# Decoder trunk: the merge's broadcast loads on GpSimd's queue, the output projection's residual and sum of squares on VectorE, and a reordered pool

## The chip, the cores and the metric

The kernel runs on one core of a Trainium2 chip. The metric is device microseconds (us) of one execution. A core has TensorE (PE in the profile, its weight loads PEld), VectorE (DVE), ScalarE (ACT), GpSimd (POOL) and SyncE (SP). Each engine works through its own instructions in their order. SP does nothing but issue DMAs here; POOL issues DMAs too and computes a little. A DMA issued by either engine is one in that engine's queue: an issue that has to wait for a semaphore holds up all that stands behind it on its engine.

## The reference

One pre-norm block on x (2048 tokens, 1024 channels, fp32), a ReLU-squared MLP and a final norm:

```python
u = _rmsnorm(h, norm_mix_g[l])
z = jnp.einsum('bsd,dn->bsn', u, w_in[l])
q, k, v, pz, ga, gp = jnp.split(z, offs, axis=-1)
a = _attention_branch(q, k, v)          # 3 head groups (dilation 1, 4, 16), 4 heads of 64 each
p = _pool_branch(pz, w_pool_grp[l], pool_scale[l])
merged = sigmoid(ga) * (a @ w_att_out[l]) + sigmoid(gp) * (p @ w_pool_out[l])
h = h + merged @ w_out[l]
m = _rmsnorm(h, norm_mlp_g[l])
h = h + square(relu(m @ w_mlp_in[l])) @ w_mlp_out[l]
return _rmsnorm(h, norm_final_g)
```

In `_attention_branch` the outputs of the three groups are added with weights: the softmax, over the groups, of the log-sum-exp of each head's scores at each token.

## The kernel before

All products are in fp32 accuracy: each operand is split into a high and a low part (ScalarE casts the high part, VectorE subtracts for the low one, L527 and L528), and a product is three matmuls (L534 to L536). Tokens are cut into 4 chunks of C = 512, or into 2 halves of 1024. The parts in order of time:

- Queries, keys and values of group 2, the pool branch and the attention of group 2 (until about 420 us).
- A loop over the 4 chunks (L398 to L502, about 420 to 890 us): projections and attention blocks of groups 1 and 0, then the chunk's *merge*. For it VectorE works out the weights on 4 partitions (one for each head), POOL's queue writes them to DRAM (`wts_d`, L486), and six DMAs on SP's queue read them back, each row to 64 partitions (`wb`, L495, one for each of 3 groups and 2 pairs of heads). VectorE multiplies each group's output by its `wb` (L498 for group 0, L500 for the others) and adds up (L501) into `af`, which POOL's queue stores to `a_d` (L502). `wb` has three buffers, so that the fourth load waits until the first buffer has been used.
- The *B part* (L547 to L751, about 890 to 2255 us), with a pool `wp` of its own and the order gates(0), merge(0), gates(1), residual(0), merge(1), mlp_in(0), residual(1), mlp_in(1). Gates, residual and mlp_in run `stage` (L611): a matrix product in Strassen's manner, in rounds of two output pairs j, each with seven products (ORDER1). The first three products of a pair leave PSUM as tiles zA, zS, zS (L637, ScalarE copies); of the next three each is added to one of them on VectorE (L640), the seventh becomes zc, and `fin` does what is left with each of the four results. All these tiles and `fin`'s own come from one ring of buffers, tag zz, ZB = 12 of them. The names of tiles and of PSUM banks carry the stage: g gates, o output projection (residual), c first layer of the MLP; hx, h22 and tt tiles are activations, raw (r_) and s tiles are weights, w and m tiles are their split parts.
- `residual` (the stages o): `fin` adds x to z by a DMA on POOL's queue that accumulates in place (L699), stores h (L700), squares z on ScalarE (L702), adds the square into `hss_d` in DRAM by another accumulating DMA (L703), scales z in place (L704) and stores hg (L705).
- The MLP's second layer and the final norm (pool c2, until the end).

A scheduler with a simulated timeline sets the order of instructions on each engine, by priority and by the times that it works out for them; a tile that takes a buffer over waits for the last use of the tiles that were there. Pools are laid out in SBUF in the order in which tags first appear, so that a tag's place decides which earlier tiles its first buffers lie over.

Of the kernel before, what the change touches and what calls it, by code (L numbers as in the profile page):

```python
# [12 lines left out]
ALU = mybir.AluOpType  # L13
# [6 lines left out]
KD = D // P  # L20
# [27 lines left out]
def trunk_kernel(ctx: ExitStack, tc, xt, w_qk, w_v, w_pz, w_grp, w_gates, w_att, w_pool, w_o, w_1, w_2, cols, out):  # L48
    nc = tc.nc
# [16 lines left out]
    mg_d = dram.tile([KD, P, SEQ], F32, name="mg_d")  # L66
    hg_d = dram.tile([KD, P, SEQ], F32, name="hg_d")
    hss_d = dram.tile([NCH, P, C], F32, name="hss_d")
# [11 lines left out]
    g_mix, g_mlp, g_fin = colt[:, 0:KD], colt[:, KD:2 * KD], colt[:, 2 * KD:3 * KD]  # L80
# [135 lines left out]
    for half in range(2):  # L216
        grp = fold.tile([96, 2, 2, 192], F32, name=f"grp{half}", tag="grp", bufs=2)
        nc.sync.dma_start(grp, w_grp[half])
        for quarter in range(4):
            wz = fold.tile([96, 2, 2, 256], F32, name=f"wz{half}_{quarter}", tag="wz", bufs=4)  # L220
            nc.sync.dma_start(wz, w_pz[half, quarter])
            for k in (2 * quarter, 2 * quarter + 1):
                ps = ps_a1(f"fold{half}_{k}")
# [5 lines left out]
                src = ps[:, :384].rearrange("p (n j) -> p n j", n=3)  # L229
# [11 lines left out]
    with ExitStack() as st:  # L241
        a1 = pool_of(st, "a1")
        wqk, wv = [], []
        for c in range(NCH):
            cs = slice(c * C, (c + 1) * C)
            ssq = a1.tile([P, C], F32, name=f"ssq{c}", tag="ssq", bufs=2)
# [100 lines left out]
    with ExitStack() as st:  # L347
# [4 lines left out]
        for c in range(NCH):  # L352
            u = gained_x(c, f"a2_{c}")
            for n in range(6):
                w = split_load(w_pzg_d[n], D, f"wz{c}_{n}", lo_on=nc.gpsimd)
                ps = ps_mm(f"a2_{c}_{n}")
# [3 lines left out]
                z = zext[n]  # L360
# [37 lines left out]
    for c in range(NCH):  # L398
        u = xh, xl = norm_x(c, f"a3_{c}")
        ot, negm, ll = {}, {}, {}  # L400
        for g in (1, 0):
            qk = []
            for i in range(4):
                w = split_load(w_qk[4 * g + i], D, f"a3_{c}_{g}_{i}")
                ps = ps_mm(f"a3_{c}_{g}_{i}")
                mm3_chunk(ps, w, u)
                t = a3p.tile([P, C], F32, name=f"qk_{c}_{g}_{i}", tag=f"q{g}" if i < 2 else f"k{g}",
                             bufs=2 if i < 2 else 4)
# [8 lines left out]
            for t in range(4):  # L417
                ps = ps_mm(f"a3v_{c}_{g}_{t}")
# [71 lines left out]
        for g in range(3):  # L490
            for hp in range(2):
                wb = mg.tile([P, C], F32, name=f"wb_{c}_{g}_{hp}", tag="wb", bufs=3)
                src = bass.AP(tensor=wts_d.tensor, offset=wts_d[c, g, 2 * hp].offset,
                              ap=[[C, 2], [0, HD], [1, C]])
                nc.sync.dma_start(wb, src)  # L495
                o = (o2c if g == 2 else ot[g])[:, hp, :]
                if g == 0:
                    nc.vector.tensor_mul(af[:, hp, :], wb, o)  # L498
                else:
                    nc.vector.tensor_mul(wb, wb, o)  # L500
                    nc.vector.tensor_add(af[:, hp, :], af[:, hp, :], wb)  # L501
# [46 lines left out]
    wp = pool_of(wps, "wp")  # L548
    COMBS = ("B11", "T1", "T2", "B22", "T3", "B21", "T4")
    ORDER1 = ("A11 B11 b", "S1 T1 c", "S2 T2 b", "S4 B22 c", "S3 T3 b", "A12 B21 a", "A22 T4 b")  # L550
    RAWB, SB, WB, ZB = 4, 5, 5, 12

    def wtile(name, tag="zz", bufs=ZB):
        return wp.tile([P, C], F32, name=name, tag=tag, bufs=bufs)

    def load_act(src, k, t, hf, key, tag="hx", bufs=3):

# [50 lines left out]
            raw.append(r)  # L608
        return [r[:, i * C:(i + 1) * C] for r in raw for i in range(2)]

    def stage(key, weights, n_pairs, make, fin, extra=None):  # L611


        m = {}
        for j0 in range(0, n_pairs, 2):
            js = (j0, j0 + 1)
            w, bank, mid = {}, {}, {}
            for j in js:
                a11, a12, a21, a22 = raws((weights[2 * j], weights[2 * j + 1]), f"{key}_{j}")
                s1, s2, s3, s4 = sums(a11, a12, a21, a22, f"{key}_{j}")  # L620
                w[j] = {"A11": a11, "A12": a12, "A22": a22, "S1": s1, "S2": s2, "S3": s3, "S4": s4}
            for n, step in enumerate(ORDER1):
                a, b, bk = step.split()
                if j0 == 0:
                    m[b] = make(b)
                for j in js:
                    kj = f"{key}_{j}"
                    wh, wl = split(wp, w[j][a], f"{kj}_{a}", "w", WB)
                    first = (j, bk) not in bank
                    if first:  # L630
                        bank[j, bk] = ps_c(f"{kj}_{bk}")
                    ps = bank[j, bk]
                    mm_acc(ps, [(wh[:, k * P:(k + 1) * P], wl[:, k * P:(k + 1) * P], *m[b][k])
                                for k in range(KH)], first, True)
                    if n in (0, 1, 2):
                        t = mid[j, n] = wtile(f"z{a}_{kj}")
                        nc.scalar.copy(t, ps)  # L637
                    elif n < 6:
                        t = mid[j, {3: 2, 4: 1, 5: 0}[n]]
                        nc.vector.tensor_add(t, ps, t)  # L640
                        fin(j, *{3: (0, 1), 4: (1, 1), 5: (0, 0)}[n], t, None)
                    else:
                        fin(j, 1, 0, wtile(f"zc_{kj}"), ps)
            if extra:
                extra(j0 // 2)

    def at(hf, t):
        return slice(hf * HT + t * C, hf * HT + (t + 1) * C)
# [43 lines left out]
                nc.gpsimd.dma_start(mg_d[e, :, at(hf, t)], z)  # L692

    def residual(hf):
        def fin(j, row, t, z, ps):
            e, c = 2 * j + row, 2 * hf + t
            if ps is not None:
                nc.scalar.copy(z, ps)
            nc.gpsimd.dma_start(z, xt[c, :, e, :], accum_op=ALU.add)  # L699
            nc.gpsimd.dma_start(h_d[e, :, at(hf, t)], z)  # L700
            sq = wtile(f"sq_{c}_{e}")
            nc.scalar.square(sq, z)  # L702
            nc.gpsimd.dma_start(hss_d[c], sq, **({"accum_op": ALU.add} if (j, row) != FIRST else {}))  # L703
            nc.scalar.mul(z, z, g_mlp[:, e:e + 1])  # L704
            nc.gpsimd.dma_start(hg_d[e, :, at(hf, t)], z)  # L705

        FIRST = (0, 0)
        stage(f"o{hf}", w_o, KD // 2, inputs(mg_d, hf, f"o{hf}"), fin)


    def mlp_in(hf):
# [217 lines left out]
```

## Time and profile before

| | |
|---|---|
| median of 3 runs | 2917.45 us (2913.21 to 2920.82) |
| profiled execution | 2918.79 us |
| its span | 2916.7 us |
| PE / DVE / ACT / POOL busy, share of the span | 91% / 62% / 46% / 14% |

A row of instructions in the profile's views reads: start or group, engine, line, operation, output<-input by the program's names with the buffer numbers left out, tile sizes, and how often (x). In a timeline the first two numbers are start and duration in us, and square brackets give how long the engine was idle ahead of it and what ended that. A row of waits reads: engine, what it was about to do, what it waited for; us in total, times, longest. A row of windows has the stretch, its length, the busy time of PE, PEld, DVE, ACT and POOL with the number of instructions, the TensorE clock that was granted (1 is 2.4 GHz, 0.5 is 1.2 GHz), the share of the 16 DMA engines' time, and GB/s.

### The profile page before, as it was taken

The page shows a single profiled execution, that of the slowest core. Times are in us where ns is not written, and L with a number is a line of the kernel's source. Part 1 is how long each engine was busy: PE and PEld are TensorE (multiplying, and loading weights), DVE is VectorE, ACT ScalarE, POOL GpSimd, SP SyncE. Part 2 cuts the span into 40 slices and gives each one's busy share as a digit, 9 for nine tenths or more (in the row PEclk, how much of TensorE's full clock was granted, in tenths as well). Part 3 has the DMA queues.
Part 4 walks back from the last instruction along what each step waited for, and adds up shares of the span by engine and source line. Part 5 has one row for each costly group of instructions (what it writes and reads, how often), then busy time and mean ns, then how long its engine had stood idle before and what let it go on. Part 6 is the DMA issues. An engine that isn't in the chain of part 4 may idle for free.

```text
span 2916.7 us, 37152 instructions
## 1 busy us (share of the span) xinstructions
PE 2652.3 (91%) x12966; PEld 2177.2 (75%) x12966; DVE 1815.4 (62%) x2848; ACT 1355.0 (46%) x2504; POOL 405.8 (14%) x617
## 2 busy tenths in 40 slices
PE   8999999788727999997999999769999999999996
PEld 7887788677625887886678887658887788878885
DVE  5469847555447457574576667466665584787557
ACT  5444444334325433454335556455555544464444
POOL 3024300000000110113302221332222000000000
PEclk9999999899868999998899999889999999999998
DMA  7234544422106465357955556785555946683433
GB/s 254 82 111 163 175 171 145 137 80 98 55 24 200 130 228 180 131 186 181 305 183 199 188 188 208 194 222 188 188 188 201 329 124 193 206 268 105 127 111 127
DMA packets 207948, 493.92 MB, mean 169 GB/s; under 512 B 26672, under 2 KB 33840, under 8 KB 207632
## 3 DMA queue, kind: packets, MB, share of 16 engines
q1 hardware_dynamic: 160128, 347.75, 37.7%
q0 software_dynamic: 47632, 143.79, 14.6%
q8 instruction: 102, 1.67, 0.2%
q14 instruction: 86, 0.70, 0.1%
HBM read 347.68 MB, written 143.75 MB: 168 GB/s over the span
## 4 chain that ended last, share of the span: by engine, by line
PE 47%; issue 35%; DMA 9%; DVE 4%; POOL 3%; ACT 1%; SPq 0%; POOLq 0%; DVEq 0%; ACTq 0%
PE z L535 6%; PE z L536 6%; PE z L534 6%; PE z_c_b L534 3%; PE z_c_b L536 3%; PE z_c_b L535 3%; PE z_c_c L534 2%; PE z_c_c L536 2%; PE z_c_c L535 2%; PE mm_v L275 2%; DMA x<-hid_d 1%; POOL sg_d L654 1%; PE mm L125 1%; PE mm L126 1%; PE mm L127 1%
## 5 line engine op out<-in xcount | busy, mean ns | idle before, releaser
L528 DVE TENSOR_TENSOR wl_S<-r_S,wh_S 128x512 fp32r<-128x512 f32 x128 | 88.3, 690 | 123.5 <-ACT wh_S L527 123.5
L527 ACT CAST wh_S<-r_S 128x512 fp32r<-128x512 f32 x128 | 79.9, 624 | 182.1 <-PE z L535 162.6
L535 PE MATMUL z<-xl_T,wh_S 128*128 128x512 f32 x384 | 149.6, 390 | 2.8 <-DVE xl_T L528 2.8
L316 ACT ACTIVATE sb_g<-sb_g,negm 128x256 f32<-128x256 f32 (+1 forms) x192 | 86.2, 451 | 136.4 <-DVE negm L314 136.4
L536 PE MATMUL z<-xh_T,wl_S 128*128 128x512 f32 x384 | 149.4, 389 | 0.0
L528 DVE TENSOR_TENSOR wl_c_S<-s_c,wh_c_S 128x512 fp32r<-128x512 f32 x128 | 86.8, 688 | 94.7 <-ACT wh_c_S L527 94.5
L534 PE MATMUL z<-xh_T,wh_S 128*128 128x512 f32 x384 | 135.7, 389 | 0.0
L527 ACT CAST wh_c_S<-s_c 128x512 fp32r<-128x512 f32 x128 | 77.2, 616 | 75.9 <-PE z_c_c L535 41.0
L321 PE MATMUL t_g<-ident,sb_g 128*128 128x128 f32 x300 | 67.0, 315 | 43.9 <-ACT sb_g L316 43.4
L527 ACT CAST wh_A<-r_A 128x512 fp32r<-128x512 f32 x96 | 59.5, 620 | 98.8 <-PE z L535 62.0
L528 DVE TENSOR_TENSOR wl_A<-r_A,wh_A 128x512 fp32r<-128x512 f32 x96 | 65.8, 687 | 59.2 <-ACT wh_A L527 58.5
L126 PE MATMUL mm_a<-xl_a,hi_a 128*128 128x512 f32 x256 | 102.4, 401 | 0.0
L535 PE MATMUL z<-xl_B,wh_A 128*128 128x512 f32 x256 | 100.5, 393 | 1.5 <-DVE xl_B L528 1.5
L127 PE MATMUL mm_a<-xh_a,lo_a 128*128 128x512 f32 x256 | 101.9, 398 | 0.0
L125 PE MATMUL mm_a<-xh_a,hi_a 128*128 128x512 f32 x256 | 99.8, 398 | 1.4 <-ACT qk L410 1.4
L534 PE MATMUL z<-xh_B,wh_A 128*128 128x512 f32 x256 | 94.2, 400 | 6.5 <-ACT xh_B L527 5.8
L536 PE MATMUL z<-xh_B,wl_A 128*128 128x512 f32 x256 | 98.2, 392 | 0.0
L798 POOL TENSOR_TENSOR y<-y,frs 128x256 f32<-128x256 f32 x4 | 3.2, 825 | 650.9 <-DVE frs L146 650.9
L527 ACT CAST wh_c_A<-r_c 128x512 fp32r<-128x512 f32 x96 | 59.5, 620 | 69.2 <-PE z_c_b L535 27.1
L535 PEld LDWEIGHTS z<-xl_T,wh_S 128*128 128x128 f32 x384 | 72.1, 188 | 18.6 <-DVE xl_T L528 3.7
L528 DVE TENSOR_TENSOR wl_c_A<-r_c,wh_c_A 128x512 fp32r<-128x512 f32 x96 | 65.8, 685 | 29.7 <-ACT wh_c_A L527 29.7
L534 PEld LDWEIGHTS z<-xh_T,wh_S 128*128 128x128 f32 x384 | 72.1, 188 | 15.1
(503 smaller groups left out, 8681.0 us busy)
## 6 DMA issues: line engine op xcount, KB each, us to landing
x<-hid_d SPq DMA_DIRECT2D x160, 256.0 KB
r_c<-in_w SPq DMA_DIRECT2D x64, 512.0 KB
r_S<-w2s_d SPq DMA_DIRECT2D x128, 256.0 KB
x_a<-in_xt SPq DMA_DIRECT2D x96, 256.0 KB
r_A<-in_w SPq DMA_DIRECT2D x96, 256.0 KB
raw_a<-in_w_qk SPq DMA_DIRECT2D x32, 512.0 KB
r_g<-in_w_gates SPq DMA_DIRECT2D x32, 512.0 KB
r_w<-in_w SPq DMA_DIRECT2D x32, 512.0 KB
```

The lines of the kernel that those rows point to most:

```text
L125: nc.tensor.matmul(ps, lh, rh, start=(i == 0), stop=False)
L126: nc.tensor.matmul(ps, lh, rl, start=False, stop=False)
L127: nc.tensor.matmul(ps, ll, rh, start=False, stop=(i == n - 1))
L275: nc.tensor.matmul(pv[t][:, :256], a, b, start=(k == 0 and n == 0), stop=(k == KD - 1 and n == 2))
L316: nc.scalar.activation(s[:, h, :W], s[:, h, :W], AF.Exp, bias=negm[:, col + h:col + h + 1], accum_out=l[:, col + h:col + h + 1])
L321: nc.tensor.transpose(ps_t[:, b, h * P:(h + 1) * P], s[:, h, b * P:(b + 1) * P], ident)
L527: nc.scalar.copy(hi, src)
L528: nc.vector.tensor_sub(lo, src, hi.bitcast(F32))
L534: nc.tensor.matmul(ps, lh, rh, start=start and i == 0, stop=False, skip_group_check=True)
L535: nc.tensor.matmul(ps, lh, rl, start=False, stop=False, skip_group_check=True)
L536: nc.tensor.matmul(ps, ll, rh, start=False, stop=stop and i == n - 1, skip_group_check=True)
L654: nc.gpsimd.dma_start(sg_d[2 * j + row, :, at(hf, t)], z)
```

## The change

1. The 24 `wb` loads (L495) are issued on GpSimd's queue in place of SP's.
2. In `wp` the ring zz has 11 buffers in place of 12, a new tag ssq has two, and both are allocated ahead of all others, so that they take the pool's lowest addresses; raw, s, hx and the rest move up.
3. In `residual`, SP's queue loads the chunk of x into the z tile ahead of the product, and VectorE adds PSUM to it (`onto`; 32 loads and 32 adds), where ScalarE copied PSUM out (32 copies) and POOL's queue accumulated x (32 DMAs). VectorE sums the squares in the ssq tiles (28 adds), with four stores of them to `hss_d`, where 32 DMAs did it. The scaled copy goes to a tile of its own (hg) from zz.

```diff
-                nc.sync.dma_start(wb, src)
+                nc.gpsimd.dma_start(wb, src)
...
-    RAWB, SB, WB, ZB = 4, 5, 5, 12
+    RAWB, SB, WB, ZB = 4, 5, 5, 11
...
+    for tag, bufs in (("zz", ZB), ("ssq", 2)):
+        wtile(f"first_{tag}", tag, bufs)
...
-    def stage(key, weights, n_pairs, make, fin, extra=None):
+    def stage(key, weights, n_pairs, make, fin, extra=None, onto=None):
...
                     if n in (0, 1, 2):
                         t = mid[j, n] = wtile(f"z{a}_{kj}")
-                        nc.scalar.copy(t, ps)
+                        if onto:
+                            nc.sync.dma_start(t, onto(j, *((0, 0), (1, 1), (0, 1))[n]))
+                            nc.vector.tensor_add(t, ps, t)
+                        else:
+                            nc.scalar.copy(t, ps)
...
     def residual(hf):
+        ssq = [wtile(f"ssq_{hf}_{t}", "ssq", 2) for t in range(2)]
+
+        def onto(j, row, t):
+            return xt[2 * hf + t, :, 2 * j + row, :]
+
         def fin(j, row, t, z, ps):
-            e, c = 2 * j + row, 2 * hf + t
+            e = 2 * j + row
             if ps is not None:
-                nc.scalar.copy(z, ps)
-            nc.gpsimd.dma_start(z, xt[c, :, e, :], accum_op=ALU.add)
+                nc.sync.dma_start(z, onto(j, row, t))
+                nc.vector.tensor_add(z, ps, z)
             nc.gpsimd.dma_start(h_d[e, :, at(hf, t)], z)
-            sq = wtile(f"sq_{c}_{e}")
-            nc.scalar.square(sq, z)
-            nc.gpsimd.dma_start(hss_d[c], sq, **({"accum_op": ALU.add} if (j, row) != FIRST else {}))
-            nc.scalar.mul(z, z, g_mlp[:, e:e + 1])
-            nc.gpsimd.dma_start(hg_d[e, :, at(hf, t)], z)
-
-        FIRST = (0, 0)
-        stage(f"o{hf}", w_o, KD // 2, inputs(mg_d, hf, f"o{hf}"), fin)
+            if e == 0:
+                nc.scalar.square(ssq[t], z)
+            else:
+                sq = wtile(f"sq_{hf}_{t}_{e}")
+                nc.scalar.square(sq, z)
+                nc.vector.tensor_add(ssq[t], ssq[t], sq)
+            g = wtile(f"hg_{hf}_{t}_{e}")
+            nc.scalar.mul(g, z, g_mlp[:, e:e + 1])
+            nc.gpsimd.dma_start(hg_d[e, :, at(hf, t)], g)
+
+        stage(f"o{hf}", w_o, KD // 2, inputs(mg_d, hf, f"o{hf}"), fin, onto=onto)
+        for t in range(2):
+            nc.gpsimd.dma_start(hss_d[2 * hf + t], ssq[t])
```

The change moves instructions at three places. First SP's queue at the end of the last chunk's merge, where the first loads of the gates' weights (r_g) and activations (hx_g_B) follow; before:

```order
L488 DMA o2c_7228<-o_d 128x2x512
L495 DMA wb_0_0_7231<-wts_d 128x1x512
L495 DMA wb_0_1_7234<-wts_d 128x1x512
L495 DMA wb_1_0_7237<-wts_d 128x1x512
L495 DMA wb_1_1_7241<-wts_d 128x1x512
L495 DMA wb_2_0_7245<-wts_d 128x1x512
L495 DMA wb_2_1_7249<-wts_d 128x1x512
L607 DMA r_g_0_0_7267<-in_w_gates 128x1024
L607 DMA r_g_0_1_7269<-in_w_gates 128x1024
```

The same place on SP after the change:

```order
L431 DMA v_3_3_6578<-v_d_64 128x256
L488 DMA o2c_7228<-o_d 128x2x512
L611 DMA r_g_0_0_7269<-in_w_gates 128x1024
L611 DMA r_g_0_1_7271<-in_w_gates 128x1024
L611 DMA r_g_1_0_7281<-in_w_gates 128x1024
L611 DMA r_g_1_1_7283<-in_w_gates 128x1024
L563 DMA hx_g_B_0_0_7293<-u_d 128x512
```

Before, the gates' first loads stand behind the six wb loads, which wait for `wts_d`; now they stand behind o2c alone. The wb loads are on POOL's queue now, between the store that they wait for and the store of the merge's result:

```order
L486 DMA wts_d<-nm_7158 4x3x512
L495 DMA wb_0_0_7231<-wts_d 128x1x512
L495 DMA wb_0_1_7234<-wts_d 128x1x512
L495 DMA wb_1_0_7237<-wts_d 128x1x512
L495 DMA wb_1_1_7241<-wts_d 128x1x512
L495 DMA wb_2_0_7245<-wts_d 128x1x512
L495 DMA wb_2_1_7249<-wts_d 128x1x512
L502 DMA a_d<-af_7230 128x1024
```

Only stores of later work stand behind them there. The third place is the first residual stage, from its first round (pairs 0 and 1) to its second (2 and 3); ScalarE before, where the two names of a tile in L704 are one tile:

```order
L702 ACTIVATE sq_1_11185<-zc_o_0_11181 128x512
L698 COPY zc_o_1_11206<-z_o_1_b 128x512
L527 CAST wh_o_2_S_11399<-s_o_2_11221 128x512
L704 ACTIVATE zc_o_0_11181<-zc_o_0_11181,colt 128x512
L702 ACTIVATE sq_3_11210<-zc_o_1_11206 128x512
L637 COPY zA_o_2_11256<-z_o_2_b 128x512
L637 COPY zA_o_3_11275<-z_o_3_b 128x512
```

VectorE at that place after the change:

```order
L720 TENSOR_TENSOR ssq_0_10705<-ssq_0_10705,sq_0_1_11191 128x512
L713 TENSOR_TENSOR zc_o_1_11213<-z_o_1_b,zc_o_1_11213 128x512
L528 TENSOR_TENSOR wl_o_2_S_11328<-s_o_2_11228,wh_o_2_S_11327 128x512
L604 TENSOR_TENSOR s_o_3_11241<-r_o_3_0_11235,r_o_3_1_11237 128x512
L720 TENSOR_TENSOR ssq_0_10705<-ssq_0_10705,sq_0_3_11217 128x512
L528 TENSOR_TENSOR wl_o_3_S_11347<-s_o_3_11240,wh_o_3_S_11346 128x512
L644 TENSOR_TENSOR zA_o_2_11264<-z_o_2_b,zA_o_2_11264 128x512
L644 TENSOR_TENSOR zA_o_3_11284<-z_o_3_b,zA_o_3_11284 128x512
```

What empties the PSUM banks of pairs 2 and 3 (zA_o_2, zA_o_3) stood on ScalarE behind the squares of zc, and stands on VectorE behind the sums now; it also has the load of x as an input.

## Rows read from the trace of the kernel before

**Rows 1.** Page, busy time of TensorE: us, share of the span, instructions.

```profile
PE 2652.3 (91%) x12966; PEld 2177.2 (75%) x12966; DVE 1815.4 (62%) x2848; ACT 1355.0 (46%) x2504; POOL 405.8 (14%) x617
```

**Rows 2.** Waits of TensorE in the whole span.

```profile
PE z_g_b L534 <- ACT mB11h_g L527: 60.3, 1, 60.3
PE t_g L321 <- ACT sb_g L316: 43.4, 10, 8.3
PE z_o_b L534 <- ACT zA_o L637: 26.1, 2, 13.7
PE z_c_b L534 <- ACT zA_c L637: 21.5, 1, 21.5
PE o_g L329 <- ACT ot L331: 16.5, 3, 5.9
```

**Rows 3.** Windows around the merges of chunks 0, 1 and 2.

```profile
500.00:560.00 60.00, 41.75 (x292) 36.41 (x291) 27.85 (x42) 20.78 (x45) 2.37 (x5) 0.83 0.25 85
640.00:680.00 40.00, 21.95 (x149) 20.44 (x150) 14.59 (x24) 11.08 (x27) 1.13 (x2) 0.74 0.24 85
765.00:800.00 35.00, 18.23 (x125) 16.59 (x127) 10.21 (x17) 8.24 (x22) 0.58 (x1) 0.66 0.17 64
```

**Rows 4.** VectorE's waits for tile wb in all four merges: us, times.

```profile
  DMA wb<-wts_d: 109.8, 24
```

**Rows 5.** Timeline of the last chunk's merge and the start of the gates.

```profile
847.04 20.12 SPq L495 DMA_DIRECT2D wb<-wts_d  x6
854.61 0.69 DVE L498 TENSOR_TENSOR af<-wb,ot 128x512 f32<-128x512 f32 x1 [10.51 <-DMA wb<-wts_d]
859.88 0.69 DVE L498 TENSOR_TENSOR af<-wb,ot 128x512 f32<-128x512 f32 x1 [4.58 <-DMA wb<-wts_d]
865.24 0.69 DVE L500 TENSOR_TENSOR wb<-wb,ot 128x512 f32<-128x512 f32 x1 [4.67 <-DMA wb<-wts_d]
...
870.58 0.69 DVE L500 TENSOR_TENSOR wb<-wb,ot 128x512 f32<-128x512 f32 x1 [3.92 <-DMA wb<-wts_d]
...
876.71 0.69 DVE L500 TENSOR_TENSOR wb<-wb,o2c 128x512 f32<-128x512 f32 x1 [5.45 <-DMA wb<-wts_d]
...
884.09 0.69 DVE L500 TENSOR_TENSOR wb<-wb,o2c 128x512 f32<-128x512 f32 x1 [5.48 <-DMA wb<-wts_d]
...
885.13 0.62 ACT L527 CAST wh_g_A<-r_g 128x512 fp32r<-128x512 f32 x1 [49.39 <-DMA r_g<-in_w_gates]
...
890.32 1.22 PE L534 MATMUL z_g_b<-mB11h_g,wh_g_A 128*128 128x512 f32 x2 [60.25 <-ACT mB11h_g L527]
```

**Rows 6.** Window in which little but wb loads moves.

```profile
850.00:870.00 20.00, 0.00 (x0) 0.00 (x0) 2.77 (x4) 0.00 (x0) 0.00 (x0) 0.50 0.13 49
```

**Rows 7.** The accumulating loads of x, L699, POOL's queue: issue to landing.

```profile
DMA to landing us min/median/max: 4.1/7.1/11.1
```

**Rows 8.** The stores u_d, L176, POOL's queue: issue to landing.

```profile
DMA to landing us min/median/max: 2.6/5.1/10.2
```

**Rows 9.** Windows of residual(0), two, and residual(1), two.

```profile
1330.00:1380.00 50.00, 37.60 (x156) 30.57 (x155) 17.76 (x27) 20.96 (x36) 22.61 (x32) 0.86 0.88 210
1380.00:1440.00 60.00, 52.97 (x201) 39.61 (x200) 31.38 (x51) 30.13 (x53) 24.62 (x35) 0.86 0.98 278
1860.00:1900.00 40.00, 26.31 (x110) 21.30 (x109) 11.40 (x17) 18.37 (x33) 15.76 (x23) 0.83 0.89 208
1900.00:1960.00 60.00, 34.91 (x138) 27.69 (x137) 36.52 (x58) 31.12 (x55) 22.50 (x31) 0.78 0.94 245
```

**Rows 10.** ScalarE's timeline in residual(0), ahead of the second round's first copy.

```profile
1371.26 0.63 ACT L702 ACTIVATE sq<-zc_o 128x512 f32<-128x512 f32 x1 [1.59 <-DMA zc_o<-in_xt]
1371.80 1.05 ACT L637 COPY zA_o<-z_o_b 128x512 f32<-128x512 f32 x2
```

**Rows 11.** Start of c2: SP's first weight load, and mlp_in(1)'s last group of stores.

```profile
2241.25 0.33 SPq L763 DMA_DIRECT2D r_A<-in_w  x1
L715 POOL DMA_DIRECT2D hid_d<-zc_c x32: 539/542/542, 1547.9 to 2254.4; - x32
```

## The prediction

> **What bounds the kernel now.** I began with the page's busy times: TensorE works 2652.3 us of the span of 2916.7 [rows 1]. The change takes no matmul away, so it can only win back what TensorE stands idle, 264 us, and what it runs slowly after standing idle. Next I read TensorE's waits. Five groups matter here [rows 2]: one wait of 60.3 us for the gates' first activation; 43.4 us and 16.5 us in the attention loop for ScalarE's exponentials (sb_g) and outputs (ot); 26.1 us in the residual stages and 21.5 us just behind the second, for the copy zA that empties a PSUM bank. Then I asked, by timeline and windows, what stands behind each.
>
> In the attention loop the releaser named is ScalarE, but the cause is VectorE: it works in order, its part of the attention blocks stands among the merge's multiplications, and these wait for wb. The 24 waits for wb sum to 109.8 us [rows 4]. Of these the last merge has six, 10.51 + 4.58 + 4.67 + 3.92 + 5.45 + 5.48 = 34.6 us [rows 5], so each of the others has 75.2 / 3 = 25.1 us. Around those three merges TensorE stands idle 60 - 41.75 = 18.3, 40 - 21.95 = 18.1 and 35 - 18.23 = 16.8 us [rows 3], 53 us together. The granted clock there is 0.83, 0.74 and 0.66, that is 20.4, 20.8 and 23.8 us at the lower level, 65 us in all. If all idle time lay in these, 12 us of work ran at half speed and lost 6 us; if none, 65 us did and lost 32. The middle is 19: the merges cost TensorE 53 + 19 = 72 us.
>
> The 60.3 us are the last chunk's: no next chunk covers its merge. The first wb load is issued at 847.04 and used at 854.61, 7.6 us later, and then one comes every 4.6 to 6.7 us, as if one after another; the last addition ends at 884.81 + 0.69 = 885.5 and the first matmul of the gates starts at 890.32 [rows 5]. While little else moves, all 16 DMA engines are busy 0.13 of the time on average, that is two of them, with 49 GB/s [rows 6]: six loads of 256 KB share two engines.
>
> In the residual stages the copies of zA stand on ScalarE behind a square that waits for POOL's accumulating load of x [rows 10].
>
> **The change part by part.** The sum is made against the profiled execution's 2918.8 us, 1.3 us above the median of the runs.
>
> *Merges of chunks 0 to 2.* The first load still needs its 7.6 us, and each merge keeps its first wait, some 5.6 us of the 25.1. POOL's queue shows transfers overlapping: in the window of 50 us POOL issues 32 instructions, nearly all of them DMAs [rows 9], one every 1.6 us, while a DMA of the same 256 KB takes 4.1 to 11.1 us there, 7.1 in the median [rows 7]. So I take it that three loads issued together land 7.6 us later and close together. The second three wait for the buffers of the first, and one more wait of about 5 us is left. Saved: 25.1 - 5.6 - 5 = 14.5 us of 25.1, 0.58 of 72 = **42 us**. No row shows a broadcast load on this queue, so the bounds are wide. From below nothing saved, or a loss, where loads land one after another at 7.1 to 11.1 us; from above they land as fast as POOL's fastest store of a tile of this size, 2.6 us [rows 8], and 21 of 25.1 us go, 60 us. I take the middle because the one duration of such a load that I have is 7.6 us, and two engines for each load would hold on any queue. VectorE's order there keeps the same instructions, shifted by a few places. The wb loads that wait for a buffer now hold POOL's queue; behind them stand the merge's own store and stores of u_d, which are read in the gates only, so that costs nothing.
>
> The Trainium skill (DMA: Bandwidth & Descriptors, section "Why a DMA increments its semaphore by 16 and not by 1") gives a reason for the two engines: a transfer uses the largest number of engines up to 16 that divides the slowest dimensions of both patterns, and a hardware queue takes the lowest-numbered ones. The source's slowest dimension is 2 here, so every load on SP's queue has the same two; the share of 0.13 agrees [rows 6]. For GpSimd's queue it says that the engines are taken in turn, and on trn2 all 16 for some direct copies, which no row here shows. By the turn the sum is the one below; by all 16 it is the first rival.
>
> *End of the last merge.* By the same reckoning the first three loads land near 854.6. Their buffers are free at about 855.3, 856.5 and 857.8, the second three land 7.6 us on, at 863 to 865.4, and the last addition ends at about 866.9 instead of 885.5: 18.6 us. The gates' first weights are no longer behind the wb loads on SP; before, ScalarE waited for them until 885.13 [rows 5], which is beside the merge's end, and the 4.8 us from there to the first matmul shrink by about 2, as the loads of activations come early too. Sum **21 us**. Bounds: 2 to 6 us if the wb loads stay as slow; 31 us if they land in 2.6 us (28.5 + 2). What is late next is VectorE's own chain (weights' differences and sums, then the split of the first activation).
>
> *Residual stages.* The windows give idle times of 12.4, 7.0, 13.7 and 25.1 us [rows 9], and by the same working as above lost clock of about 2.5, 6, 1.7 and 3 us. With x loaded ahead by SP, the squares wait for VectorE alone and the banks are emptied by VectorE behind nothing that waits for a DMA but the load of x itself, which is issued when the ring gives a buffer. The second round's first tile takes the buffer of the first round's zA, so its load waits for that tile's store to land; rows don't tell whether it lands ahead of the need, and I take it that it just does. I credit all of the first window (15 us), 4 of the 13 in the second, where casts for merge(1) are waited for too, 13 of 15.4 in the third, and 20 of 28 in the fourth, where mlp_in's first copies stood behind the squares [rows 2]. **52 us**. Bounds: 20, if the loads of x come late in the second round, and 65. VectorE gets 32 + 28 adds at about 0.69 us, 41 us; in these windows it is busy 17.8 of 50, 31.4 of 60, 11.4 of 40 and 36.5 of 60 us [rows 9], so they fit. ScalarE loses 32 copies at 0.53, 17 us, and POOL 60 DMAs; neither bounds anything.
>
> *Layout and the ring of 11.* The new low zz buffers lie where c2's first weight tiles will be. SP issues the first weight load at 2241.25, while mlp_in(1)'s last store goes out at 2254.4 [rows 11]. The first loads of c2 may have to wait for late stores. Bounds 0 to 12 us lost; TensorE has work queued at that point, so I take **4 us** lost. One buffer less I cost at nothing: TensorE's largest waits name no tile that waits for a buffer of the ring [rows 2].
>
> Sum: 42 + 21 + 52 - 4 = 111; 2918.8 - 111 = 2807.8, and 1.3 less for the median: about 2807 us.
>
> **Rivals.**
> (a) The wb loads land in about 2.6 us, spread over many engines. For it: POOL's fastest store [rows 8]; against it: the source is two rows for 64 readers each. 60 + 31 + 52 - 4 = 139, 2778 us.
> (b) The queue makes no difference: the loads still share two engines, one every 5.3 us. For it: the limit is seen on the DMA engines [rows 6], not at the issue. Then the merges give 0, the end of the last one 4: 4 + 52 - 4 = 52, 2865 us. The skill's same page, section "Issuing engines are not separate DMA queues", speaks for this case: all issuers' transfers run on the same 16 engines, and another issuer saves only issue time.
> (c) Loads of x block SP's queue in the residual stages. They wait for zz buffers, and the weights r_o and merge(1)'s inputs stand behind them. For it: hg tiles now take zz buffers too, and there are 11. Then the residual term falls to about 15: 42 + 21 + 15 - 4 = 74, 2843 us.
> (d) Slower: on POOL's queue the wb loads land strictly one after another, as slowly as that queue's slow loads. Six loads then take 6T against the 37 us from 847.04 to 884.09, in all four merges, against 52 - 4 = 48 us of gain: it decides from T = (48 / 4 + 37) / 6 = 8.2 us. At 11.1 us [rows 7] it costs 4 x (66.6 - 37) = 118 us, and the time is 2917.5 + 70 = 2987 us. Against it: POOL's transfers overlap in rows 9.
>
> **How the numbers follow.** Forecast 0.44, (a) 0.26, (b) 0.12, (c) 0.11, (d) 0.07. A measurement of this kernel can tell about 0.3%, 9 us, from no change. (b) and (c) together, with the whole 12 us lost at c2's start, would leave about no change, and I give that 0.02 of their chance. Faster 0.91, same 0.02, slower 0.07. The likeliest's own range is 2790 to 2830. The range of 8 in 10 reaches from a little below (a), 2765, to a little above (b), 2875; the rest of the chance lies mostly in (d).
>
> **What would show it.** Right: VectorE's waits for wb near 11 us in a merge; the gates' first matmul some 22 us after the last merge's first wb load is issued, where 890.32 - 847.04 = 43 stand now; no wait of TensorE for zA above a few us in the o stages; square's wait for in_xt gone. Wrong: wb landing one every 5.3 us again (b); one wait of 2 to 4 us per triple (a); long idle times on SP ahead of x loads, with wh_o waiting for r_o behind them (c); POOL's landings of wb near 8 us apart (d); a TensorE wait above 10 us at the start of c2 (layout).

## The result, and the profile after

The changed kernel takes 2831.55 us in the median of 4 runs (2828.03 to 2838.14), the kernel before 2916.18 (2913.21 to 2920.82): a ratio of 0.9711, 95% interval 0.9688 to 0.9734, so 84.6 us or 2.9% faster. The forecast was 2807, its range 2765 to 2875; the range given to the likeliest case alone, 2790 to 2830, is missed by 1.6 us. The two profiled executions take 2828.03 and 2918.79 us, 90.8 us apart.

Where these went is read best by position in TensorE's work. Both kernels have 12966 TensorE instructions, in nearly one order, so I compared the starts of instructions of equal number. What a stretch takes less than before, in us, worked out from the traces (numbers in the first column bound the stretch; start of its first instruction in the trace before):

```
instructions, from us     what lies there          after  e1_wb  e2_layout  e3_resid  n2_nolayout
0 to 2750,    6           until chunk 0's merge     -1.4   -0.9    -1.9      -1.1      -2.4
2750 to 3250, 499         merge of chunk 0         -12.8  -12.0    -0.2      +1.0     -10.7
3250 to 4000, 593         merge of chunk 1          -6.2   -6.0     0.0      +0.7      -7.3
4000 to 4500, 715         merge of chunk 2         -10.2  -12.3    -0.1      +0.4     -13.6
4500 to 5000, 800         last merge, gates start  -16.7  -17.4    +0.7       0.0     -16.2
6500 to 7500, 1312        residual(0)              -21.2   -0.2     0.0     -23.0     -22.9
8500 to 9250, 1808        residual(1)              -25.9   -3.8    -2.8     -25.2     -24.2
10000 to 10750, 2205      start of c2               +5.6   -0.7    +7.0      -0.4      +0.7
```

The four other columns are experiments told below. In the changed kernel three merges give 29.2 us, the last one's end 16.7, the residual stages 47.1, and the start of c2 takes 5.6 back. (The first row moves by 1 to 2.4 us from run to run with nothing changed there, and that of residual(1) by 3.8 in e1_wb, which leaves the residual stages alone: so much of that row is not clear of noise.)

TensorE's waits after the change, to be held against [rows 2]:

```profile
PE z_g_b L534 <- ACT mB11h_g L527: 41.7, 1, 41.7
PE t_g L321 <- ACT sb_g L316: 15.7, 9, 4.6
PE o_g L329 <- ACT ot L331: 11.5, 2, 10.3
...
PE z_o_b L534 <- ACT wh_o_A L527: 9.7, 1, 9.7
PE s_g L307 <- DVE sb_g L311: 9.6, 5, 3.9
...
PE z_c_b L534 <- ACT zA_c L646: 8.2, 1, 8.2
```

The wait for zA in the o stages, 26.1 us, is gone from the list's head; that for zA_c fell from 21.5 to 8.2, the gates' from 60.3 to 41.7. In the attention loop 43.4 + 16.5 us of [rows 2], with 1.8 us for sb_g of VectorE that stand further down the same list, 61.7 in all, became 15.7 + 11.5 + 9.6 = 36.8. What is left of the wait for zA_c is ScalarE's order: it reaches the copy 8 us after a cast that waited for hg to come back from DRAM, with other casts, squares and scalings between.

```profile
1852.50 0.62 ACT L527 CAST mB22h_c<-h_c_T 128x512 fp32r<-128x512 f32 x1 [3.65 <-DMA h_c_T<-hg_d]
...
1860.74 1.05 ACT L646 COPY zA_c<-z_c_b 128x512 f32<-128x512 f32 x2
```

The end of the last merge, by the timeline, to be read beside [rows 5]:

```profile
815.67 2.38 POOL L495 DMA_DIRECT2D wb<-wts_d  x3 [2.20 <-DMA wts_d<-nm]
823.62 1.29 DVE L498 TENSOR_TENSOR af<-wb,ot 128x512 f32<-128x512 f32 x2 [11.05 <-DMA wb<-wts_d]
824.60 1.58 POOL L495 DMA_DIRECT2D wb<-wts_d  x2 [6.55 <-DVE af L498]
825.89 0.69 DVE L500 TENSOR_TENSOR wb<-wb,ot 128x512 f32<-128x512 f32 x1 [0.98 <-DMA wb<-wts_d]
...
827.60 0.79 POOL L495 DMA_DIRECT2D wb<-wts_d  x1 [1.42 <-DVE af L501]
832.50 0.69 DVE L500 TENSOR_TENSOR wb<-wb,ot 128x512 f32<-128x512 f32 x1 [5.19 <-DMA wb<-wts_d]
...
836.43 0.69 DVE L500 TENSOR_TENSOR wb<-wb,o2c 128x512 f32<-128x512 f32 x1 [1.19 <-DMA wb<-wts_d]
837.15 0.69 DVE L501 TENSOR_TENSOR af<-af,wb 128x512 f32<-128x512 f32 x1
...
840.27 1.22 PE L534 MATMUL z_g_b<-mB11h_g,wh_g_A 128*128 128x512 f32 x2 [41.75 <-ACT mB11h_g L527]
843.56 0.79 PE L535 MATMUL z_g_b<-mB11l_g,wh_g_A 128*128 128x512 f32 x1 [2.07 <-DVE mB11l_g L528]
```

Three loads go out within 2.4 us and the first lands 8 us later, the second with it, the third 2 us behind: two rounds of 8 us, where six loads came one every 5.3 us or more. From the first load's issue to the gates' first matmul are 24.6 us (43.3 before). The window in which these three loads are under way, one in which only the last load of the second round is, and the landings of all 24 (issue to landing):

```profile
818.00:823.00 5.00, 0.00 (x0) 0.00 (x0) 0.00 (x0) 0.00 (x0) 0.05 (x1) 0.50 0.41 127
834.00:835.00 1.00, 0.00 (x0) 0.00 (x0) 0.96 (x2) 0.00 (x0) 0.00 (x0) 0.50 0.13 49
```

```profile
DMA to landing us min/median/max: 7.4/8.2/9.2
```

With three loads under way the DMA engines are 0.41 busy, 6.6 of 16, at 127 GB/s, where [rows 6] has 0.13 and 49. One load alone has 0.13 and 49 here too, two engines: a load is no wider than before, but loads have engines of their own. VectorE's waits for wb in all merges are 65.8 us in place of the 109.8 of [rows 4]:

```profile
  DMA wb<-wts_d: 65.8, 15
```

The last merge has 11.05 + 0.98 + 5.19 + 1.19 = 18.4 of them. The first wait of each of the three others, before:

```profile
517.08 0.69 DVE L498 TENSOR_TENSOR af<-wb,ot 128x512 f32<-128x512 f32 x1 [5.64 <-DMA wb<-wts_d]
639.95 0.69 DVE L498 TENSOR_TENSOR af<-wb,ot 128x512 f32<-128x512 f32 x1 [5.71 <-DMA wb<-wts_d]
762.75 0.69 DVE L498 TENSOR_TENSOR af<-wb,ot 128x512 f32<-128x512 f32 x1 [5.75 <-DMA wb<-wts_d]
```

And after, with the issue of each merge's first three loads:

```profile
510.25 2.41 POOL L495 DMA_DIRECT2D wb<-wts_d  x3 [4.12 <-issue]
517.99 1.29 DVE L498 TENSOR_TENSOR af<-wb,ot 128x512 f32<-128x512 f32 x2 [6.74 <-DMA wb<-wts_d]
...
617.95 2.40 POOL L495 DMA_DIRECT2D wb<-wts_d  x3 [2.19 <-DMA wts_d<-nm]
627.14 0.69 DVE L498 TENSOR_TENSOR af<-wb,ot 128x512 f32<-128x512 f32 x1 [7.82 <-DMA wb<-wts_d]
...
734.52 2.40 POOL L495 DMA_DIRECT2D wb<-wts_d  x3 [2.19 <-DMA wts_d<-nm]
743.27 0.69 DVE L498 TENSOR_TENSOR af<-wb,ot 128x512 f32<-128x512 f32 x1 [10.73 <-DMA wb<-wts_d]
```

The first waits have grown.

In residual(0), the place of [rows 10], VectorE now empties the banks; its timeline at the step from first to second round:

```profile
1302.08 0.69 DVE L713 TENSOR_TENSOR zc_o<-z_o_b,zc_o 128x512 f32<-128x512 f32 x1
1302.68 0.68 DVE L528 TENSOR_TENSOR wl_o_S<-s_o,wh_o_S 128x512 fp32r<-128x512 f32 x1
1303.40 0.69 DVE L604 TENSOR_TENSOR s_o<-r_o,r_o 128x512 f32<-128x512 f32 x1
...
1305.76 1.40 DVE L644 TENSOR_TENSOR zA_o<-z_o_b,zA_o 128x512 f32<-128x512 f32 x2 [0.43 <-DMA zA_o<-in_xt]
...
1803.12 0.69 DVE L713 TENSOR_TENSOR zc_o<-z_o_b,zc_o 128x512 f32<-128x512 f32 x1 [3.12 <-DMA zc_o<-in_xt]
```

The load of x into the reused buffer is late by 0.43 us. Of the other 31 VectorE waits for two, 0.46 us and, in residual(1), 3.12. At the start of c2, SP's timeline. Before, the second weight load follows the first of [rows 11] at once:

```profile
2242.17 0.39 SPq L763 DMA_DIRECT2D r_A<-in_w  x1
```

After:

```profile
2151.81 0.33 SPq L782 DMA_DIRECT2D r_A<-in_w  x1
...
2157.89 0.33 SPq L782 DMA_DIRECT2D r_A<-in_w  x1
...
2163.59 0.33 SPq L782 DMA_DIRECT2D r_A<-in_w  x1
```

The first three weight loads stand 6 us apart, where 0.9 us lay between the first two, and SP's waits name what they wait for:

```profile
SPq L782 <- DMA hid_d<-zd: 11.3, 1, 11.3
SPq L782 <- DMA hid_d<-zS_c: 5.1, 1, 5.1
```

These are mlp_in(1)'s last stores out of zz buffers, which the new order put under c2's weights.

### The profile page after: what moved, and what is told of

It is laid out like the page before. It is cut to its first block, busy times and chain, and to the rows that moved or that the text cites. A ratio compares the mean times of both kernels' runs of the same rounds, so it can differ in the third digit from the quotient of the medians.

```text
span 2826.3 us, 37148 instructions
## 1 busy us (share of the span) xinstructions
PE 2643.4 (94%) x12966; PEld 2170.3 (77%) x12966; DVE 1849.3 (65%) x2908; ACT 1337.5 (47%) x2472; POOL 369.6 (13%) x581
## 4 chain that ended last, share of the span: by engine, by line
PE 51%; issue 27%; DMA 10%; DVE 6%; POOL 4%; ACT 2%; SPq 0%; POOLq 0%; DVEq 0%; ACTq 0%
PE z L535 6%; PE z L536 6%; PE z L534 6%; PE z_c_b L534 2%; PE z_c_b L535 2%; PE z_c_b L536 2%; DMA wb<-wts_d 2%; PE mm_v L275 2%; POOL hid_d L734 1%; DMA x<-hid_d 1%; PE z_g_b L535 1%; PE z_g_b L536 1%; PE z_g_b L534 1%; PE mm L127 1%; PE mm L125 1%
## 5 line engine op out<-in xcount | busy, mean ns | idle before, releaser
L535 PEld LDWEIGHTS z<-xl_T,wh_S 128*128 128x128 f32 x384 | 72.1, 188 | 18.6 <-DVE xl_T L528 3.7
L527 ACT CAST wh_g_S<-s_g 128x512 fp32r<-128x512 f32 x64 | 39.4, 620 | 98.8 <-DVE s_g L601 36.0
L536 PEld LDWEIGHTS z<-xh_T,wl_S 128*128 128x128 f32 x384 | 72.1, 188 | 14.9
```

The costliest lines, as they stand in the source:

```text
L527: nc.scalar.copy(hi, src)
L535: nc.tensor.matmul(ps, lh, rl, start=False, stop=False, skip_group_check=True)
L536: nc.tensor.matmul(ps, ll, rh, start=False, stop=stop and i == n - 1, skip_group_check=True)
```

## Experiments: the three parts one by one

Each kernel was timed in turn with the kernel before on the same chip. Four chips were used, on which the kernel before takes 2916.1 to 2918.5 us in the median, so kernels timed on different ones are best compared by their ratios to it. The edit of *e1_wb* on the kernel before:

```diff
-                nc.sync.dma_start(wb, src)
+                nc.gpsimd.dma_start(wb, src)
```

> The kernel before with part 1 alone: the wb loads on GpSimd's queue. Theory (queue): the loads of a triple land together, 7.4 to 9.2 us after issue, on engines of their own; the three inner merges give back 12.4 + 6.8 + 10.7 = 30 us as between the two traces and the end of the last merge about 17, together some 47 us: 2870 us. Rival (layout): the early end of the last merge needs the weights' buffers of part 2 as well, since without it the first gates' weights lie over tiles that the attention still uses; then 17 us stay away and it is about 2887. Rival (queue makes nothing): 2913 to 2917, landings 5.3 us apart.

Measured: 2863.79 us, ratio 0.9811 (0.9795 to 0.9826). The queue theory holds in each row of the table: 30.3 us in three merges and 17.4 at the end of the last. The layout is not needed for that end.

*e2_layout*, on the kernel before:

```diff
-    RAWB, SB, WB, ZB = 4, 5, 5, 12
+    RAWB, SB, WB, ZB = 4, 5, 5, 11
...
+    for tag, bufs in (("zz", ZB), ("ssq", 2)):
+        wtile(f"first_{tag}", tag, bufs)
```

> The kernel before with part 2 alone: ring of 11, zz and ssq first in the pool (ssq allocated and not used). Theory: it gains nothing at the start of the gates, since the first weights still stand behind the wb loads on SP's queue, and it costs at the start of c2, where the two traces differ by 5.7 us: about 2922 us. Rival (the layout pays): weights load before the merge's end and 3 to 10 us are gained: 2907 to 2914.

Measured: 2922.28 us, ratio 1.0018 (1.0006 to 1.0030), slower by a little; the loss stands where it was expected, 7.0 us at the start of c2, and nothing is gained at the gates. SP's waits there show the same two stores, TensorE's a wait for c2's first activations of up to 7.8 us:

```profile
SPq L767 <- DMA hid_d<-zd: 10.7, 1, 10.7
SPq L767 <- DMA hid_d<-zS_c: 6.4, 1, 6.4
```

```profile
PE z L534 <- ACT xh_B L527: 12.0, 3, 7.8
```

*e3_resid* is the kernel before with `onto`, the adds, ssq and hg of part 3, and the ring of 11 without the new order.

> The kernel before with part 3 alone (x loaded by SP, adds and sum of squares on VectorE, hg in tiles of its own; ring of 11 so that it fits, old order of the pool's tags). Theory: the residual stages give back what the two traces differ by there, 22.5 and 26 us, about 48 us, and nothing else moves: 2868 us. Rival (a ring of 11 with hg in it is too small without the layout): loads of x wait for buffers, half of it goes: about 2892.

Measured: 2874.89 us, ratio 0.9851 (0.9833 to 0.9869). The stages give 23.0 and 25.2 us, as in the whole change; the ring of 11 is not too small. The three parts alone, 52.3, -6.2 and 41.2 us in medians, sum to 87.3, against 84.6 together: they hardly touch each other.

*n2_nolayout*, on the changed kernel:

```diff
-    for tag, bufs in (("zz", ZB), ("ssq", 2)):
-        wtile(f"first_{tag}", tag, bufs)
```

> The changed kernel without the order of the pool's tags (first_zz and first_ssq taken out, ring of 11 kept). Theory: the start of c2 gets its 5.7 us back and the start of the gates stays, since the first weights are loaded long before the merge ends either way: about 2825 us, 6 below the changed kernel. Rival (the layout pays at the gates): the start of the gates comes later by some us, 2831 to 2838.

Measured: 2822.75 us (2820.62 to 2824.95), ratio to before 0.9670 (0.9654 to 0.9685); the changed kernel has 0.9711. c2 starts without the loss, with SP's first four weight loads between 2144.70 and 2148.82 us, and the gates lose nothing. So it is the order of the tags that costs, not the ring of 11, which both have.

## Experiments: what the broadcast loads wait for

*sp_split* leaves the loads of the kernel before on SP's queue and changes only the pattern, which cuts each load in two:

```diff
-                src = bass.AP(tensor=wts_d.tensor, offset=wts_d[c, g, 2 * hp].offset,
-                              ap=[[C, 2], [0, HD], [1, C]])
-                nc.sync.dma_start(wb, src)
+                for par in range(2):
+                    src = bass.AP(tensor=wts_d.tensor, offset=wts_d[c, g, 2 * hp + par].offset,
+                                  ap=[[0, HD], [1, C]])
+                    nc.sync.dma_start(wb[par * HD:(par + 1) * HD], src)
```

> The kernel before, wb loads left on SP's queue; each load is cut into two, one for each head, so that each reads one DRAM row for 64 partitions (48 loads of 128 KB). Theory (the loads of before share two DMA engines because the pattern's slowest dimension is 2; a pattern that begins with 64 spreads over all 16): VectorE's waits for wb fall from 109.8 us to about 30, the share of the DMA engines while they load is well above 0.13, the inner merges give 50 to 60 us and the last one's end about 20: 2836 to 2846 us. Rival (SP's queue does such loads one after another whatever their shape, or the one DRAM row read 64 times is the limit): landings stay 5.3 us apart for 256 KB and the time stays at 2916.

Measured: 2822.01 us, ratio 0.9678 (0.9655 to 0.9700): this edit alone gives more than the whole change, and more than I expected by 14 us. SP's issues (ns, min/median/max), landings, the timeline of the last merge and the window of its loads:

```profile
L496 SPq DMA_DIRECT2D wb<-wts_d x48: 444/590/599, 509.2 to 782.2; - x48
...
DMA to landing us min/median/max: 2.7/3.0/4.7
```

```profile
773.58 9.24 SPq L496 DMA_DIRECT2D wb<-wts_d  x12
777.28 0.69 DVE L499 TENSOR_TENSOR af<-wb,ot 128x512 f32<-128x512 f32 x1 [6.62 <-DMA wb<-wts_d]
778.44 0.69 DVE L499 TENSOR_TENSOR af<-wb,ot 128x512 f32<-128x512 f32 x1 [0.47 <-DMA wb<-wts_d]
780.29 0.69 DVE L501 TENSOR_TENSOR wb<-wb,ot 128x512 f32<-128x512 f32 x1 [1.16 <-DMA wb<-wts_d]
...
785.22 0.69 DVE L501 TENSOR_TENSOR wb<-wb,o2c 128x512 f32<-128x512 f32 x1 [0.75 <-DMA wb<-wts_d]
```

```profile
772.00:783.00 11.00, 0.00 (x0) 0.00 (x0) 4.02 (x6) 0.00 (x0) 0.00 (x0) 0.50 0.42 123
```

Twelve half loads go out on SP's queue in 9.24 us, one of 128 KB every 0.77 us, of which the issue itself is 0.59; some wait a little for one of the three buffers. On two engines at the 49 GB/s of [rows 6] each would take 2.7 us. Each lands 2.7 us or more after its issue, so several are under way at once on this queue, and the engines' share is 0.42. So neither SP's queue nor the DRAM row that is read 64 times was the limit; the pattern was. The edit halves each load and takes the slowest dimension of 2 away at once; a whole load with 64 as its slowest dimension was not tried. VectorE's waits for wb fall to 16.3 us in all four merges, and the three inner merges give 25.0 + 24.6 + 24.0 = 73.6 us, the last one's end 21.4, where the gates' weights still come behind the wb loads.

*n_b6*, on n2_nolayout, loads uncut on GpSimd's queue:

```diff
-                wb = mg.tile([P, C], F32, name=f"wb_{c}_{g}_{hp}", tag="wb", bufs=3)
+                wb = mg.tile([P, C], F32, name=f"wb_{c}_{g}_{hp}", tag="wb", bufs=6)
```

> The kernel n2_nolayout (2822.75 us) with six wb buffers instead of three, on GpSimd's queue. Theory (the forecast's merge term was too large because the second triple waits for buffers, with another 8 us to land): VectorE's waits for wb fall from 65.8 us in the changed kernel to 36 or less, the last addition of the last merge comes some 9 us sooner, the inner merges give about 20 us: 2793 us. Rival (the rest of the merges' loss is not the wait for wb but VectorE's own order): under 8 us, 2815 to 2823.

Measured: 2799.74 us, ratio 0.9595 (0.9579 to 0.9611), 23 us below n2_nolayout. The three inner merges give 50.0 us, where n2_nolayout has 10.7 + 7.3 + 13.6 = 31.6, so 18.4 more, near the 20 of the theory. The waits for wb fall to 42.6 us, 6.6 more than expected, and the last addition of the last merge ends 16.9 us after the first issue, where it was 21.6: 5 us sooner and not 9. Six loads at once land later:

```profile
DMA to landing us min/median/max: 8.3/10.1/11.0
```

So the second round of 8 us, for want of buffers, held the merge term down; the first wait stays.

The last four combine these on n2_nolayout: cut loads on either queue, with three or six buffers.

> The kernel n2_nolayout with the wb loads back on SP's queue, cut into two for each head, three buffers. Theory (it is the number of engines for each load that counts, not the queue): at least as fast as on GpSimd's queue with two engines each, 2793 to 2805 us. Rival (the queue is what counts, and SP's loses the gates' early weights): 2850 to 2865 us, as the changed kernel without part 1.

> The kernel n2_nolayout with loads cut into two for each head, on GpSimd's queue, six buffers. Theory: first load lands about 3 us after issue; POOL needs 12 x 0.8 us to issue them, so the last lands 12 to 13 us after the first issue instead of 20: 2785 to 2795 us, within 8 us of n_b6. Rival (issue time on POOL bounds twelve loads): slower than n_b6 by over 8 us.

> The kernel n2_nolayout with wb loads cut into two for each head, on SP's queue, six buffers: n_split_pool6 but for the queue. Theory (with 16 engines for each load, what is left of the queue's choice is the gates' first weights, which on SP stand behind the wb loads): inner merges as in n_split_sync, the end of the last merge 4 us later than in n_split_pool6, so 2770 to 2780 us. Rival (the 11 us between n_split_sync and n_split_pool6 come from the buffers alone): 2764 to 2769 us.

> The kernel n2_nolayout with wb loads cut into two for each head, on GpSimd's queue, three buffers. With n_split_sync and n_split_sync6 (both 2779 us) and n_split_pool6 (2768 us) it crosses queue and buffers. Theory (the queue makes the 11 us, not the buffers): 2766 to 2772 us. Rival (on GpSimd's queue, with its longer issue, three buffers are not enough): 2775 to 2790 us.

```
                  three buffers                             six buffers
SP's queue        2779.38, ratio 0.9524 (0.9510, 0.9538)    2779.25, ratio 0.9526 (0.9510, 0.9542)
GpSimd's queue    2773.03, ratio 0.9503 (0.9489, 0.9518)    2768.41, ratio 0.9491 (0.9473, 0.9509)
```

With cut loads the buffers no longer matter on SP's queue, and the queue matters little. n_split_sync came out 14 us below what was expected, n_split_pool6 17 us below, n_split_sync6 inside its theory's span, n_split_pool just above its own and short of its rival's. Whether GpSimd's queue is better by 6 to 11 us or by less stays open: the profiled executions of n_split_sync6 and n_split_pool6 take 2774.9 and 2775.3 us. By position, as in the table above, the end of the last merge gives 27.0 and 25.4 us on GpSimd's queue (six and three buffers) and 24.0 and 23.3 on SP's, so 2 to 3 us there speak for GpSimd's, in the direction of the theory of the gates' early weights. In the sum they are hidden by rows where these two do not differ in the code: the first takes 4.3 us more in n_split_pool6 and residual(1) 3.7. All four beat both kernels; the one with the lowest median, n_split_pool6, is 2.2% below the changed kernel (2768.41 / 2831.55).

## Experiments: which half of part 3

*r1_xonly* is e3_resid with the end of `fin` as before, *r2_sqonly* with its start as before:

```diff
 r1_xonly
...
-            if e == 0:
-                nc.scalar.square(ssq[t], z)
-            else:
-                sq = wtile(f"sq_{hf}_{t}_{e}")
-                nc.scalar.square(sq, z)
-                nc.vector.tensor_add(ssq[t], ssq[t], sq)
-            g = wtile(f"hg_{hf}_{t}_{e}")
-            nc.scalar.mul(g, z, g_mlp[:, e:e + 1])
-            nc.gpsimd.dma_start(hg_d[e, :, at(hf, t)], g)
+            sq = wtile(f"sq_{hf}_{t}_{e}")
+            nc.scalar.square(sq, z)
+            nc.gpsimd.dma_start(hss_d[2 * hf + t], sq, **({"accum_op": ALU.add} if (j, row) != (0, 0) else {}))
+            nc.scalar.mul(z, z, g_mlp[:, e:e + 1])
+            nc.gpsimd.dma_start(hg_d[e, :, at(hf, t)], z)
...
 r2_sqonly
-                nc.sync.dma_start(z, onto(j, row, t))
-                nc.vector.tensor_add(z, ps, z)
+                nc.scalar.copy(z, ps)
+            nc.gpsimd.dma_start(z, onto(j, row, t), accum_op=ALU.add)
...
-        stage(f"o{hf}", w_o, KD // 2, inputs(mg_d, hf, f"o{hf}"), fin, onto=onto)
+        stage(f"o{hf}", w_o, KD // 2, inputs(mg_d, hf, f"o{hf}"), fin)
```

> The kernel before with half of part 3: x loaded by SP and added by VectorE; the squares still summed by accumulating DMAs, the scaled copy in place (ring of 11, old order of tags). Theory (the banks were emptied late because a square ahead on ScalarE waited for POOL's accumulating load of x): most of part 3's 41 us, 2875 to 2885 us. Rival (the accumulating DMAs of the squares, each waiting for the one before, hold POOL's queue and the ring's buffers): less than half, 2895 to 2912 us.

> The kernel before with the other half of part 3: the squares summed by VectorE and the scaled copy in a tile of its own; x still added by POOL's accumulating DMAs, PSUM copied out by ScalarE (ring of 11, old order of tags). Theory: the square still waits for the accumulating load ahead of the copy, little is gained, 2905 to 2917 us. Rival (the squares' DMAs were the cause): 2875 to 2890 us.

Measured: r1_xonly 2889.89 us, ratio 0.9900 (0.9886 to 0.9915); r2_sqonly 2911.36, ratio 0.9978 (0.9968 to 0.9989). The load of x carries 28.6 of part 3's 41 us, the sum of squares and hg alone 7 (3 to 9 by the interval), and in r2_sqonly TensorE waits for zA as before:

```profile
PE z_o_b L534 <- ACT zA_o L642: 26.5, 2, 13.4
PE z_c_b L534 <- ACT zA_c L642: 20.7, 1, 20.7
```

r1_xonly missed its span by 5 us. By position its profiled execution, the slowest of its four, lacks 11.0 us of e3_resid's gain in residual(0), 5.9 in residual(1) and 3.9 at the start of c2. In the residual stages what it lacks is seen on ScalarE, where the scaling in place waits for the store of h out of the same tile,

```profile
ACT zS_o L712 <- DMA h_d<-zS_o: 21.2, 11, 4.2
```

and at the start of c2 TensorE waits up to 8.4 us for the sum of squares, hss, which is 1.4 in e3_resid:

```profile
PE z_st L136 <- DMA hss<-hss_d: 9.3, 2, 8.4
```

The two halves together (41) are worth a little more than their sum (36). Both waits are seen; how much of the 5 us each makes was not tried by itself.

## Why the prediction was right, and which term was too large

The direction, the places and the main mechanisms came out as argued; the time is 24.5 us above the forecast, because of sizes. All four terms were off to the same side, towards too much gain, so no error made up for another.

```
term                      forecast   traces (after - before)   part alone
merges of chunks 0 to 2      -42          -29.2                  -30.3   e1_wb
end of the last merge        -21          -16.7                  -17.4   e1_wb
residual stages              -52          -47.1                  -48.2   e3_resid
layout, start of c2           +4           +5.6                   +7.0   e2_layout
sum                         -111          -87.4 of 90.8 in all
```

- **Merges.** The price of the waits was nearly right: 72 us were worked out for the 75.2 us of waits in the three. In sp_split 16.3 us of waits are left in all, 6.62 + 0.47 + 1.16 + 0.75 = 9.0 of them in the last merge and so 7.3 in the three; for what went the price gives 65 us, and 73.6 came. Some luck is in that: 19 of the 72 were the middle between 6 and 32. That two engines serve a load on either queue, and that loads on POOL's queue overlap, was right: 0.13 of the engines for one load, 0.41 for three. The step that failed is the wait that was left, "some 5.6 us" and "one more wait of about 5 us", 10.6 in a merge. It is (65.8 - 18.4) / 3 = 15.8 us. The larger half of the excess is in the first wait: 6.74, 7.82 and 10.73 us, 8.4 in the mean instead of 5.6. The first load is used 7.7, 9.2 and 8.8 us after its issue instead of 7.6, which is 1 us of it. The rest is that VectorE runs out of other work sooner, where its order was taken to be "shifted by a few places" at no cost: it begins to wait 1.0 and 1.4 us after the issue and in the third merge 2.0 us ahead of it, and before it was 1.9 us after in each. Why its other work ends sooner was not tried. All later waits are 7.4 us in a merge instead of 5: loads take 8.2 us in the median, not 7.6, and the buffers for the second three come free late, because VectorE's other work stands between their uses. With 9.3 of 25.1 us saved instead of 14.5 the step gives 0.37 x 72 = 27 us, and 29.2 were measured. n_b6 shows the later waits from the other side: with six buffers the inner merges give 16.0 + 18.1 + 15.9 = 50 us.
- **End of the last merge.** Two rounds of loads, as forecast: 837.15 + 0.69 - 815.67 = 22.2 us from issue to the last addition's end, where 866.9 - 847.04 = 19.9 were worked out. The same 0.6 us a load and the later buffers make the difference. TensorE's wait fell by 60.3 - 41.7 = 18.6 us; the stretch gives less, 16.7, because some is lost again behind the gates' first matmul, where TensorE now waits 2.07 us for VectorE's split of the first activation (0.8 before), the chain that the prediction had named as late next. (Its "4.6 to 6.7 us" between the loads should read 5.3 to 7.4 by the uses in [rows 5]; no sum rests on it.)
- **Residual stages.** Right in sum, though not half by half: 19 us were credited to residual(0), which gave 21.2, and 33 to residual(1), which gave 25.9. The second round's load of x lands just in time as I had taken it to (late by 0.43 us). The adds fit on VectorE. The miss is the fourth window, for which 20 us were credited and where TensorE still waits 8.2 us for zA_c: the squares that waited for x are gone from ScalarE ahead of that copy, but the casts that wait for hg are not. The lost clock in this term, 2.5, 6, 1.7 and 3 us, does not come out "by the same working": the middles are 3.9, 6.6, 3.4 and 6.9. The windows held more than the prediction said.
- **Layout.** Right, and of the size taken; two stores of mlp_in(1) hold c2's first weights.
- **Rivals.** Uncut loads spread over all engines (a) did not happen: 7.4 us was the fastest landing. Loads as slow as on SP (b) are ruled out by e1_wb's 0.9811. SP blocked by loads of x (c): TensorE's one wait for wh_o_A of 9.7 us had its like before (8.7 us in two), and e3_resid kept its 48 us. One after another on POOL's queue (d): the two loads of a round that land together at 823.62 exclude it.

The Trainium skill's rule on the number of engines (DMA: Bandwidth & Descriptors, "Why a DMA increments its semaphore by 16 and not by 1") agrees with the runs that test it: two engines for an uncut load on either queue (a share of 0.13), other engines for the next load on GpSimd's, and 3 us landings once the slowest dimension is 64. That GpSimd's queue gives some copies all 16 engines was not seen for this pattern. The Trainium skill's section "Issuing engines are not separate DMA queues" of the same page would have had e1_wb gain issue time alone; the measured 52.3 us decide against it here, because the queue also chose the engines.

## What to carry to other kernels

When transfers of one pattern land one after another, read the share of the DMA engines while they alone are under way: 0.13 of 16 is two engines, and then the pattern is the thing to change, before the queue. When a wait is split into rounds by a small number of buffers, price the rounds from the landing time and the time at which the buffers really come free, behind the consumer's other work; six buffers were worth 23 us here. The consumer may also reach its first wait sooner than before: the same landing time then leaves a longer wait. An order of tags that suits a pool's start can cost at its end: look at which late stores the next pool's first loads will lie over.

## What the runs showed of the hardware that was not expected

Loads of this pattern land later the more of them are under way on GpSimd's queue: 8.2 us in the median with up to three, 10.1 with up to six. A half load of 128 KB with a slowest dimension of 64 lands in 3.0 us on SP's queue, and one goes out every 0.77 us there, 0.59 of it SP's issue. The granted clock followed the idle time back up: 0.953 over the kernel before, 0.967 over the changed one, 0.975 in n_split_pool6.
